# Norm statistics in two parts, HGRN's key multiplied later, and FFN one's norm in pieces, in a two-layer streaming trunk

## The chip, the cores and the metric

The kernel runs on one core of a Trainium2 chip. The metric is the device time of one execution in microseconds, as the median of several runs. The engines are named as in the profile: PE is TensorE, DVE is VectorE, ACT is ScalarE, POOL is GpSimd, SP is SyncE, which here only issues DMAs.

## The reference

Two groups of frames share all weights: a prompt of 1024 new frames and a sample of 32 frames that continues a running stream. Each passes a Mamba-2 SSD layer and an HGRN2 layer, and a SwiGLU FFN behind each. All numbers are float32.

```python
def rmsnorm(x, w):
    y = x * lax.rsqrt(jnp.mean(x * x, axis=-1, keepdims=True) + NORM_EPS)
    return y * w

# SSD mixer, cut: proj = h @ in_w; z, xbc, dt from proj; causal conv and silu on xbc; y from the chunked scan
yg = (y + D_skip * xs) * silu(z)
yg = rmsnorm over groups of 512 of yg, times gnorm_w
out = yg @ out_w

# HGRN mixer, cut: q, f, i, g = split(h @ in_w); forget = lb + (1 - lb) * sigmoid(f); k = 1 - forget
b = jnp.cumsum(log(forget), axis=1)          # in each chunk
qe, ke = q * jnp.exp(b), k * jnp.exp(-b)
sc = jnp.where(mask, qe @ ke.T, 0.0)
o = sc @ i + qe @ S
S = jnp.exp(last) * S + (k * jnp.exp(last - b)).T @ i
out = (rmsnorm per head of o * silu(g)) @ out_w

# trunk, for layer 0 (SSD) and layer 1 (HGRN)
x = x + mixer(rmsnorm(x, norm_w[layer]))
x = x + swiglu(rmsnorm(x, ffn_norm_w[layer]), w_gate, w_up, w_down)
# at the end
y = rmsnorm(x, final_norm_w)
```

D_MODEL is 1024, the FFN's hidden width 2816, the SSD has 32 heads of 64 in 4 groups, HGRN 8 heads of 128.

## The kernel before

The residual x lies in SBUF transposed, features on partitions, as eight tiles `acc[h][m]` of 128 features for each half `h`. Half 0 is 512 frames, half 1 the other 512 and the 32 of the sample (544, in two blocks of 272). In the profile `fixed` is the one large tile that holds x, the constants and the small buffers.

A product of float32 matrices is made of three passes (`product`, L346 to L348): weight and data are each split into a high part (`wh`, `xh`) and the rest (`wl`, `xl`). ACT rounds the high part, DVE subtracts. A result tile collects in one of five PSUM banks named `mm`, and DVE adds it into x (`accumulate`, shown as `fixed<-mm,fixed`). Scores, transposes and norm sums use three PSUM banks named `sc`.

A norm of x has two steps. The statistic (`rstd_of`, called for x by `x_stat` or by `norm`): ACT squares each of the eight tiles, DVE adds them up in `sq`, PE multiplies the sum by a matrix of ones (L369), ACT makes rsqrt as Exp(-0.5 Ln). Then for each tile the norm piece: DVE multiplies x by weight and statistic (`xf`), ACT rounds (`xn`), DVE subtracts.

**SSD layer.** Eight units (two halves, four groups) run one after another. A unit's frames go through `ssd_chunk` in chunks of 128, and tasks stand between the chunks: the z products (`ssd_z`), and the four out-projections (`ssd_out`) of the unit before. In the last unit the tasks are the four z products, then the whole norm of half 0 for FFN one (`norm`, in a high priority of 600), the four out-projections of unit six, and two first pieces of FFN one. The first four tasks (`PRE`) stand ahead of the chunks, the rest is dealt out over the chunks.

**HGRN layer.** Sixteen units (half, head). While unit i is scored, the projections of unit i+1 are made, in the order f, q, v, g. `hgrn_f` makes the log forget gate and its running sum, `hep` = exp(d) and `hem` = exp(-d), and the key `hk` = k times `hem`; `hgrn_q` makes `hq` = q times `hep`. `hgrn_scores` (L885) multiplies key and query, transposes the key and the value (L888) and copies them to `hkt` and `hvt`; `hgrn_states` (L908, L921) carries the state `hS`; `hgrn_outputs` (L933, L935) makes the output `ho`, whose own norm uses L367. Every second unit the out-projection of the two heads before (`hgrn_out`, products on `hy`) stands in between. In units (0,3) and (1,3) the last task is `x_stat` of the other half.

**FFN.** `ffn_half` runs over slabs of 256 hidden columns, in groups; the out-projections of a group are made within the next one. Its `hook`, called once in group one, is `x_stat` of the other half.

The order of instructions on each engine is made by the framework's scheduler, which starts from the program order and the priorities; each engine then runs its list in order and waits at an instruction until its inputs are there. The numbers behind names such as `hk_21829` in the lists below are the scheduler's.

Of the kernel before, what the change touches and what calls it, by code (L numbers as in the profile page):

```python
# [17 lines left out]
D = 1024  # L18
KD = D // P
# [29 lines left out]
def trunk_kernel(ctx, tc, x_prompt, x_sample, state_ssd, cache_conv, state_hgrn,  # L49
# [70 lines left out]
    def tt(out, a, b, op, eng=None):  # L120
        keep((eng or V).tensor_tensor(out=out, in0=a, in1=b, op=op))  # L121
# [593 lines left out]
    def ssd_layer(after, ws):  # L715
# [13 lines left out]
        for i, (h, g) in enumerate(units):  # L729
# [5 lines left out]
            if i + 1 < len(units):  # L735
                nh, ng = units[i + 1]
                if nh != h:
                    r = []
                    ps_ = [lambda m=m: norm_pieces(1, C_SSDN, xns[1], ((0, LEN[1]),), r[0])[m]() for m in range(KD)]
                    tasks = zs[:2] + [lambda: r.append(half_two_norm())] + zs[2:] + mixed(outs[:4], ps_) + \  # L740
                        [half_two_dt] + outs[4:]
                ct = ssd_conv_tasks(nh, ng, us[i + 1])
                tasks += ct[:EARLY]
                late = ct[EARLY:]
            else:
                tasks = zs + after[:1] + outs + after[1:]
            if i == 0:
# [8 lines left out]
            if h:  # L756
# [8 lines left out]
                act(Ss, ps, AF.Copy)  # L765
            nch = len(CHUNKS[h])
            loads = chunk_loads(h, g, 0, h == 0)
            for t in tasks[:PRE]:
# [54 lines left out]
    def hgrn_f(h, e, u):  # L823
# [27 lines left out]
        act(em[:, :L], d[:, :L], AF.Exp, scale=-1.0)  # L851
        tt(k[:, :L], k[:, :L], em[:, :L], MUL)
        u.update(k=k, ep=ep, ec=ec)

    def hgrn_q(h, e, u):
        L = LEN[h]
        q = T("ys", "hq")
        hgrn_proj(h, e, 0, silu2(q))
        stt(q[:, :L], q[:, :L], 0.5, u["ep"][:, :L], MUL, MUL)
        u["q"] = q  # L860

# [128 lines left out]
    def hgrn_layer(after):  # L990
# [7 lines left out]
        for i, (h, e) in enumerate(units):  # L998
# [21 lines left out]
            else:  # L1020
                tasks += after[1:2] + [states] + after[2:] + [outputs, rstd, gate]
            if (h, e) == (0, 3):
                tasks.append(lambda: r.append(x_stat(1, st[2])))
            if (h, e) == (0, 4):
                pieces = norm_pieces(1, C_HGN, xns[1], ((0, LEN[1]),), r[0], XN2)
            if (h, e) in ((0, 4), (0, 5), (0, 6)):
                tasks = mixed(tasks, pieces[:3])
                pieces = pieces[3:]
            if (h, e) == (1, 3):
                tasks.append(lambda: r.append(x_stat(0, st[3])))  # L1030
            if (h, e) == (1, 4):
# [19 lines left out]
    def x_stat(h, keep):  # L1051

        return rstd_of([acc[h][m][:, :LEN[h]] for m in range(KD)], BLK[h], 1.0 / D, LEN[h], keep)

# [220 lines left out]
    def ffn_half(layer, h, xn, tx, first, hook, tail, extra=()):  # L1275
# [5 lines left out]
        for gi, ng in enumerate(groups):  # L1281
            hid = []
            for i in range(ng):
# [4 lines left out]

                def gate(s=s + i, g=g, before=before, gi=gi):
                    yield from ffn_gate(layer, h, s, xn, tx, g)  # L1290
                    for d in before:
                        run(ffn_outs(*d))
                    if gi == 1 and before:
                        hook()
                    if gi and extra:
                        extra.pop(0)()
# [8 lines left out]
    def mixer_ffn(mixer, layer, wc, nxt):  # L1305
# [3 lines left out]
        h0, h1 = [ffn_head(layer, 0, s, xn[0]) for s in range(HEAD)]  # L1309
        if nxt:  # L1310
            entry = lambda: norm(0, wc, xn[0], XN)
        else:
            entry = lambda r: norm_pieces(0, wc, xn[0], BLK[0], r)
        rest = mixer([entry] + h0[:2])
        tc0 = x_combos(0, xn[0], tx[0])
# [3 lines left out]
        r = []  # L1319
        due = ffn_half(layer, 0, xn[0], tx[0], HEAD, lambda: r.append(x_stat(1, st[2])), [2])  # L1320
        kept = unsplit()
# [6 lines left out]
        if not nxt:  # L1328
            for q in range(2):
                wrow.append(st[2 + q][:, :512])  # L1330
                dma(wrow[q], final_norm_w[q * 512:(q + 1) * 512].unsqueeze(0).to_broadcast([P, 512]))
            done = [lambda g=g: finish(g, lambda: psum_mm((2, 3, 4))) for g in groups_of(0, 0, H1)]
        due = ffn_half(layer, 1, xn[1], tx[1], 1, lambda: r.append(nxt and x_stat(0, st[3])),
                       [2] if nxt else [1, 1], done)
        return due, r[0]

# [166 lines left out]
```

## Time and profile before

| | |
|---|---|
| median of 3 runs | 2859.85 us (2859.65 to 2860.43) |
| the profiled execution | 2858.78 us |
| its span in the trace | 2856.8 us |
| matmuls on PE | 19676 |
| granted TensorE clock, mean | 0.999 |

The profile has one row for a group of instructions: its line in the kernel, engine, operation, output and inputs by name, shape and count. The trace's timeline has one row for an instruction, or for some in a row of one form: start in us from the beginning of the span, duration, engine, line, and in brackets the idle time of the engine just before it with the instruction that ended it. Matmuls overlap in the pipeline, so that the duration of one is longer than the distance to the next.

### The profile page before, as it was taken

The page shows a single profiled execution, that of the slowest core. Times are in us where ns is not written, and L with a number is a line of the kernel's source. Part 1 is how long each engine was busy: PE and PEld are TensorE (multiplying, and loading weights), DVE is VectorE, ACT ScalarE, POOL GpSimd, SP SyncE. Part 2 cuts the span into 40 slices and gives each one's busy share as a digit, 9 for nine tenths or more (in the row PEclk, how much of TensorE's full clock was granted, in tenths as well). Part 3 has the DMA queues.
Part 4 walks back from the last instruction along what each step waited for, and adds up shares of the span by engine and source line. Part 5 has one row for each costly group of instructions (what it writes and reads, how often), then busy time and mean ns, then how long its engine had stood idle before and what let it go on. Part 6 is the DMA issues. An engine that isn't in the chain of part 4 may idle for free.

```text
span 2856.8 us, 48826 instructions
## 1 busy us (share of the span) xinstructions
PE 2826.3 (99%) x19676; PEld 2609.1 (91%) x19676; DVE 2132.9 (75%) x3663; ACT 1561.0 (55%) x2842; POOL 43.8 (2%) x158
## 2 busy tenths in 40 slices
PE   8999999999999999999999999999999999999998
PEld 8777788999989999999999888999988999999998
DVE  6887887787787877797777556656668877787776
ACT  6665655564653744466444666656554644455544
POOL 0000000000100000000000000000000000000000
PEclk9999999999999999999999999999999999999999
DMA  6443334444322333323333223222222332433332
GB/s 181 116 115 109 97 99 113 113 114 103 106 80 92 111 104 96 111 82 100 101 97 105 74 59 89 75 80 78 75 89 88 112 96 89 122 96 104 108 93 69
DMA packets 394516, 281.54 MB, mean 99 GB/s; under 512 B 16289, under 2 KB 382514, under 8 KB 394290
## 3 DMA queue, kind: packets, MB, share of 16 engines
q1 hardware_dynamic: 394274, 278.42, 33.6%
q8 instruction: 154, 2.52, 0.4%
q14 instruction: 72, 0.59, 0.1%
q10 hardware_dynamic: 16, 0.00, 0.0%
HBM read 270.57 MB, written 7.82 MB: 97 GB/s over the span
## 4 chain that ended last, share of the span: by engine, by line
PE 91%; DVE 5%; ACT 2%; issue 1%; DMA 1%; SPq 0%; POOL 0%; DVEq 0%; ACTq 0%; POOLq 0%
PE mm L346 18%; PE mm L348 18%; PE mm L347 18%; PE mm L1148 5%; PE mm L1146 5%; PE mm L1147 5%; PE sc L1148 4%; PE sc L1147 4%; PE sc L1146 4%; PE sc L661 1%; PE sc L650 1%; PE sc L647 1%; PE mm L1424 1%; DVE fixed L121 1%; PE sc L624 1%
## 5 line engine op out<-in xcount | busy, mean ns | idle before, releaser
L118 ACT ACTIVATE wh<-raw 128x512 fp32r<-128x512 f32 (+1 forms) x687 | 555.3, 816 | 599.1 <-PE mm L347 495.3
L346 PE MATMUL mm<-xn,wh 128*128 128x272 f32 (+2 forms) x1552 | 522.1, 337 | 2.3 <-ACT pre L118 1.3
L348 PE MATMUL mm<-xn,wl 128*128 128x272 f32 (+2 forms) x1552 | 516.6, 333 | 1.7 <-DVE wl L121 1.7
L347 PE MATMUL mm<-xn,wh 128*128 128x272 f32 (+2 forms) x1552 | 515.6, 333 | 0.0
L121 DVE TENSOR_TENSOR wl<-raw,wh 128x1024 fp32r<-128x1024 f32 (+1 forms) x307 | 373.0, 1217 | 147.3 <-ACT wh L118 118.2
L121 DVE TENSOR_TENSOR fixed<-mm,fixed 128x272 f32<-128x272 f32 (+3 forms) x504 | 259.6, 525 | 186.0 <-PE mm L348 179.7
L346 PE MATMUL mm<-fh,wh 128*128 128x272 f32 (+1 forms) x992 | 322.4, 326 | 0.3 <-ACT fh L118 0.2
L347 PE MATMUL mm<-fl,wh 128*128 128x272 f32 (+1 forms) x992 | 322.5, 326 | 0.0
L348 PE MATMUL mm<-fh,wl 128*128 128x272 f32 (+1 forms) x992 | 322.5, 326 | 0.0
L346 PEld LDWEIGHTS mm<-xn,wh 128*128 128x128 f32 x1552 | 291.5, 188 | 33.0 <-issue 2.9
L348 PEld LDWEIGHTS mm<-xn,wl 128*128 128x128 f32 x1552 | 291.4, 188 | 31.6 <-DVE wl L121 2.1
L347 PEld LDWEIGHTS mm<-xn,wh 128*128 128x128 f32 x1552 | 291.9, 188 | 27.7 <-issue 1.0
L121 DVE TENSOR_TENSOR wh<-raw,wh 128x512 fp32r<-128x512 f32 x380 | 256.3, 686 | 40.1 <-ACT wh L118 37.0
L1146 PE MATMUL mm<-th,wh 128*128 128x272 f32 (+1 forms) x912 | 260.5, 286 | 0.1
L1148 PE MATMUL mm<-th,wh 128*128 128x272 f32 (+1 forms) x912 | 259.9, 285 | 0.2 <-DVE wh L121 0.2
L1147 PE MATMUL mm<-tl,wh 128*128 128x272 f32 (+1 forms) x912 | 259.7, 285 | 0.0
L346 PEld LDWEIGHTS mm<-fh,wh 128*128 128x128 f32 x992 | 186.2, 188 | 16.4 <-ACT fh L118 1.9
L348 PEld LDWEIGHTS mm<-fh,wl 128*128 128x128 f32 x992 | 186.5, 188 | 15.4
L347 PEld LDWEIGHTS mm<-fl,wh 128*128 128x128 f32 x992 | 186.5, 188 | 15.0 <-DVE fl L121 0.2
L1146 PEld LDWEIGHTS mm<-th,wh 128*128 128x128 f32 x912 | 171.8, 188 | 1.9 <-ACT s L118 1.2
L1146 PE MATMUL sc<-xn,wh 128*128 128x272 f32 (+1 forms) x608 | 172.8, 284 | 0.5 <-ACT wh L118 0.5
L1148 PE MATMUL sc<-xn,wh 128*128 128x272 f32 (+1 forms) x608 | 173.1, 285 | 0.0
(310 smaller groups left out, 6642.6 us busy)
## 6 DMA issues: line engine op xcount, KB each, us to landing
raw<-in_ffn_w_gate_dram SPq DMA_DIRECT2D x88, 512.0 KB, 4.0
raw<-in_ffn_w_up_dram SPq DMA_DIRECT2D x88, 512.0 KB, 4.2
raw<-in_ffn_w_down_dram SPq DMA_DIRECT2D x88, 512.0 KB, 3.9
raw<-in_ssd_in_w_dram SPq DMA_DIRECT2D x80, 512.0 KB, 4.3
raw<-in_hgrn_in_w_dram SPq DMA_DIRECT2D x64, 512.0 KB, 4.0
cumB<-cumd SPq DMA_DIRECT2D x64, 256.0 KB, 4.2
raw<-in_ssd_out_w_dram SPq DMA_DIRECT2D x32, 512.0 KB, 3.4
raw<-in_hgrn_out_w_dram SPq DMA_DIRECT2D x16, 512.0 KB, 3.8
```

The source lines that it names most:

```text
L118: keep(A.activation(out=out, in_=in_, func=f, **kw))
L121: keep((eng or V).tensor_tensor(out=out, in0=a, in1=b, op=op))
L346: PE.matmul(ps[:, :bn], a, mh, start=(k == 0), stop=False)
L347: PE.matmul(ps[:, :bn], a, ml, start=False, stop=False)
L348: PE.matmul(ps[:, :bn], b, mh, start=False, stop=(k == n - 1))
L624: PE.transpose(ps[:n, j * P:(j + 1) * P], xs[j][:, xo:xo + n], ident)
L647: PE.matmul(y23[:, j, :n], S[:, j * P:(j + 1) * P], Cx, start=True, stop=True)
L650: PE.matmul(pp, Btok[:n, :], xw[:n, :], start=True, stop=True)
L661: PE.matmul(y13[r:r + 64, i // 2, :n], xdt[:n, i * 64:(i + 1) * 64], cums[i // 4][:n, i % 4, :n], start=True, stop=True)
L1146: PE.matmul(ps[:, :n], a, mh, start=(k == 0 and not more), stop=False, skip_group_check=True)
L1147: PE.matmul(ps[:, :n], a, ml, start=False, stop=False, skip_group_check=True)
L1148: PE.matmul(ps[:, :n], b, mh, start=False, stop=(k == 3), skip_group_check=True)
```

## The change

`x_stat` no longer runs as one piece. It returns a list of eight small steps, each squaring one tile (and adding it to the sum, which now lies in the buffer that later holds the statistic), and a function `mean` for the ones matmul (now L1077), Ln and Exp. The callers put the two apart:

- SSD: the squares of half 0 are mixed among unit six's tasks, `mean` stands at the start of unit seven, and the norm's eight pieces are mixed between unit six's four out-projections in unit seven, two after each, without the priority.
- HGRN: four squares among the tasks of unit e = 2, four among those of e = 3, `mean` at the end of e = 3, in both halves.
- FFN: the squares in group one, `mean` in group two.

Besides, `hgrn_f` no longer multiplies the key by exp(-d); `hgrn_q` does it behind its own multiplication. The same operations are computed on the same data; lines behind the edits move by some ten to thirty.

```diff
@@ ssd_layer
             else:
-                tasks = zs + after[:1] + outs + after[1:]
+                def entry(m):
+                    if not m:
+                        u["entry"] = after[0](u["r"])
+                    u["entry"][m]()
+                tasks = zs + mixed(outs, [lambda m=m: entry(m) for m in range(KD)]) + after[1:]
+            if i == len(units) - 2:
+                sq, mean = x_stat(0, st[0])
+                tasks = tasks[:PRE] + mixed(tasks[PRE:], sq)
...
+            if i == len(units) - 1:
+                u["r"] = mean()
             loads = chunk_loads(h, g, 0, h == 0)
@@ hgrn_f, hgrn_q
         act(em[:, :L], d[:, :L], AF.Exp, scale=-1.0)
-        tt(k[:, :L], k[:, :L], em[:, :L], MUL)
-        u.update(k=k, ep=ep, ec=ec)
+        u.update(k=k, ep=ep, em=em, ec=ec)
...
         stt(q[:, :L], q[:, :L], 0.5, u["ep"][:, :L], MUL, MUL)
+        k = u["k"]
+        tt(k[:, :L], k[:, :L], u["em"][:, :L], MUL)
@@ hgrn_layer
-            if (h, e) == (0, 3):
-                tasks.append(lambda: r.append(x_stat(1, st[2])))
+            if e in (2, 3):
+                if e == 2:
+                    sq, mean = x_stat(1 - h, st[2 + h])
+                tasks = mixed(tasks, sq[:4])
+                sq = sq[4:]
+                if e == 3:
+                    tasks.append(lambda mean=mean: r.append(mean()))
...
-            if (h, e) == (1, 3):
-                tasks.append(lambda: r.append(x_stat(0, st[3])))
@@ x_stat
-        return rstd_of([acc[h][m][:, :LEN[h]] for m in range(KD)], BLK[h], 1.0 / D, LEN[h], keep)
+        L = LEN[h]
+
+        def squares(m):
+            sq = keep if m == 0 else T("n", "sq")
+            act(sq[:, :L], acc[h][m][:, :L], AF.Square)
+            if m:
+                tt(keep[:, :L], keep[:, :L], sq[:, :L], ADD)
+
+        def mean():
+            for (b0, bn) in BLK[h]:
+                ps = psum_sc()
+                PE.matmul(ps[:, :bn], ones, keep[:, b0:b0 + bn], start=True, stop=True)
+                act(keep[:, b0:b0 + bn], ps[:, :bn], AF.Ln, bias=epsc[:, 0:1], scale=1.0 / D)
+            act(keep[:, :L], keep[:, :L], AF.Exp, scale=-0.5)
+            return keep
+        return [lambda m=m: squares(m) for m in range(KD)], mean
@@ ffn_half, in gate
-                    if gi == 1 and before:
-                        hook()
+                    if gi in (1, 2) and i == 0:
+                        hook[gi - 1]()
@@ mixer_ffn
-        if nxt:
-            entry = lambda: norm(0, wc, xn[0], XN)
-        else:
-            entry = lambda r: norm_pieces(0, wc, xn[0], BLK[0], r)
-        rest = mixer([entry] + h0[:2])
+        rest = mixer([lambda r: norm_pieces(0, wc, xn[0], BLK[0], r)] + h0[:2])
...
-        due = ffn_half(layer, 0, xn[0], tx[0], HEAD, lambda: r.append(x_stat(1, st[2])), [2])
+        sq, mean = x_stat(1, st[2])
+        due = ffn_half(layer, 0, xn[0], tx[0], HEAD, (lambda: run(sq), lambda: r.append(mean())), [2])
...
-        due = ffn_half(layer, 1, xn[1], tx[1], 1, lambda: r.append(nxt and x_stat(0, st[3])),
-                       [2] if nxt else [1, 1], done)
-        return due, r[0]
+        sq, mean = x_stat(0, st[3])
+        hooks = (lambda: run(sq), lambda: r.append(mean())) if nxt else (lambda: None,) * 2
+        due = ffn_half(layer, 1, xn[1], tx[1], 1, hooks, [2] if nxt else [1, 1], done)
+        return due, nxt and r[0]
```

How the scheduled order moves is shown at three places. The first is PE in HGRN's unit (1,3). Before, the ones matmul L369 stood among the out-projection's products (on `hy`), behind the f projection of unit (1,5):

```order
L346 MATMUL mm_17156<-hy_20104,wh_21056 128x272
L347 MATMUL mm_17156<-hy_20104,wh_21056 128x272
L348 MATMUL mm_17156<-hy_20104,wl_21057 128x272
L369 MATMUL sc_20923<-sq_20900,fixed 128x512
L885 MATMUL sc_20929<-hq_20686,hk_20644 128x128 x4
L888 MATMUL sc_20930<-fixed,hk_20644 128x128 x4
```

Now it stands, as L1077, behind the last product of the g projection (weights `wh_20854`) and ahead of the f projection of unit (1,5) (`wh_20946`), the scores (now L895) and transposes (now L898) with it:

```order
L346 MATMUL mm_17153<-h_18961,wh_20854 128x272
L347 MATMUL mm_17153<-l_18962,wh_20854 128x272
L348 MATMUL mm_17153<-h_18961,wl_20855 128x272
L1077 MATMUL sc_20917<-fixed 128x512
L895 MATMUL sc_20923<-hq_20693,hk_20649 128x128 x4
L898 MATMUL sc_20924<-fixed,hk_20649 128x128 x4
L346 MATMUL mm_17154<-h_18309,wh_20946 128x272
```

So the ones matmul, the scores and the first transposes moved ahead of the f projection and of the out-projection.

The second place is DVE in HGRN's unit (1,6), where the gates of unit (1,7) are made beside an out-projection. Before, the key's multiplication by `hem` stood ahead of a step of unit (1,6)'s state (`hS`):

```order
L124 SCALAR_TENSOR_TENSOR xf_21846<-fixed 128x512
L121 TENSOR_TENSOR hk_21829<-hk_21829,hem_21842 128x544
L921 TENSOR_SCALAR hS_21856<-fixed 128x128
L121 TENSOR_TENSOR xn<-xf_21846,xn 128x512
L121 TENSOR_TENSOR fixed<-hS_21856,sc_21851 128x128
L121 TENSOR_TENSOR fixed<-mm_17159,fixed 128x272
L921 TENSOR_SCALAR hS_21856<-fixed 128x128
```

Now the state's steps (now L931) and the accumulates (`fixed<-mm`) go on without it:

```order
L124 SCALAR_TENSOR_TENSOR xf_21839<-fixed 128x512
L931 TENSOR_SCALAR hS_21849<-fixed 128x128
L121 TENSOR_TENSOR fixed<-mm_17155,fixed 128x272
L121 TENSOR_TENSOR fixed<-hS_21849,sc_21844 128x128
L121 TENSOR_TENSOR xn<-xf_21839,xn 128x512
L931 TENSOR_SCALAR hS_21849<-fixed 128x128
L121 TENSOR_TENSOR fixed<-mm_17151,fixed 128x272
L121 TENSOR_TENSOR fixed<-mm_17152,fixed 128x272
L121 TENSOR_TENSOR fixed<-mm_17153,fixed 128x272
L121 TENSOR_TENSOR fixed<-mm_17154,fixed 128x272
L121 TENSOR_TENSOR fixed<-mm_17155,fixed 128x272
L121 TENSOR_TENSOR fixed<-mm_17151,fixed 128x272
```

The multiplication follows two rows further on, behind seven accumulates that stand in a row.

The third place is DVE in the last SSD unit. Before, the norm's `xf` and `xn` rows stood together, with two accumulates only near their end:

```order
L124 SCALAR_TENSOR_TENSOR xf_8347<-fixed,rstd_8330 128x512
L124 SCALAR_TENSOR_TENSOR xf_8351<-fixed,rstd_8330 128x512
L124 SCALAR_TENSOR_TENSOR xf_8355<-fixed,rstd_8330 128x512
L121 TENSOR_TENSOR xn<-xf_8347,xn 128x512
L121 TENSOR_TENSOR xn<-xf_8351,xn 128x512
L124 SCALAR_TENSOR_TENSOR xf_8359<-fixed,rstd_8330 128x512
L121 TENSOR_TENSOR xn<-xf_8355,xn 128x512
L124 SCALAR_TENSOR_TENSOR xf_8363<-fixed,rstd_8330 128x512
L121 TENSOR_TENSOR xn<-xf_8359,xn 128x512
L121 TENSOR_TENSOR fixed<-mm_8401,fixed 128x272
L121 TENSOR_TENSOR xn<-xf_8363,xn 128x512
L121 TENSOR_TENSOR fixed<-mm_8415,fixed 128x272
```

Now four `xn` stand ahead of the first chunk's mask product (`fixed<-sc_8284`), behind the last z products:

```order
L124 SCALAR_TENSOR_TENSOR z_8222<-z_8222,mm_8223 128x272
L121 TENSOR_TENSOR xn<-xf_8395,xn 128x512
L121 TENSOR_TENSOR xn<-xf_8399,xn 128x512
L121 TENSOR_TENSOR xn<-xf_8521,xn 128x512
L121 TENSOR_TENSOR xn<-xf_8525,xn 128x512
L121 TENSOR_TENSOR fixed<-sc_8284,fixed 128x128
L124 SCALAR_TENSOR_TENSOR xf_8647<-fixed 128x512
L124 SCALAR_TENSOR_TENSOR z_8222<-z_8222,mm_8250 128x272
L121 TENSOR_TENSOR xdt_8292<-sc_8287,fixed 128x512
L121 TENSOR_TENSOR xw_8293<-sc_8287,fixed 128x512
```

and of the other four pieces each stands among a chunk's accumulates:

```order
L121 TENSOR_TENSOR fixed<-fixed,sc_8445 128x512
L121 TENSOR_TENSOR fixed<-mm_8465,fixed 128x272
L124 SCALAR_TENSOR_TENSOR xf_8651<-fixed 128x512
L121 TENSOR_TENSOR fixed<-mm_8479,fixed 128x272
L121 TENSOR_TENSOR wl_8714<-raw_8711,wh_8713 128x1024
L121 TENSOR_TENSOR fixed<-mm_8493,fixed 128x272
L121 TENSOR_TENSOR xn<-xf_8651,xn 128x512
L124 SCALAR_TENSOR_TENSOR xf_8773<-fixed 128x512
L121 TENSOR_TENSOR fixed<-mm_8507,fixed 128x272
L121 TENSOR_TENSOR fixed<-sc_8536,fixed 128x128
```

So the accumulates no longer stand behind a row of norm pieces, and the first half of the pieces moved to the z products and the first chunk.

More of the change, by code (lines that the diff above doesn't have):

```diff
@@ L1287, in ffn_half, with gate @@
                     before, due = due, []
-                def gate(s=s + i, g=g, before=before, gi=gi):
+                def gate(s=s + i, g=g, before=before, gi=gi, i=i):
                     yield from ffn_gate(layer, h, s, xn, tx, g)
```

## The prediction

> **What bounds the kernel now.** The first view is the page's busy times and the chain of work that ended last.
>
> ```profile
> PE 2826.3 (99%) x19676; PEld 2609.1 (91%) x19676; DVE 2132.9 (75%) x3663; ACT 1561.0 (55%) x2842; POOL 43.8 (2%) x158
> PE 91%; DVE 5%; ACT 2%; issue 1%; DMA 1%; SPq 0%; POOL 0%; DVEq 0%; ACTq 0%; POOLq 0%
> ```
>
> TensorE (PE) sets the time. The change removes no matmul, so it can only give back time in which PE stands idle, or add to it. The second view is therefore the list of PE's waits; its columns are the waiting instruction, what released it, the total in us, how often, and the longest.
>
> ```profile
> PE sc L369 <- DVE sq L121: 4.9, 4, 1.8
> PE mm L212 <- DMA fixed<-in_x_prompt_dram: 4.5, 2, 4.1
> PE mm L346 <- DVE fixed L121: 2.2, 2, 1.3
> PE sc L935 <- DVE hS L921: 1.0, 1, 1.0
> PE sc L908 <- ACT hvt L118: 0.8, 1, 0.8
> ```
>
> L369 is the ones-matrix matmul of a norm: it waits until VectorE (DVE) has summed the eight squares. Of its four waits one belongs to an SSD gate, which the change leaves alone. L212 is the first load of the input and is not touched either. The other rows are. The third view, PE's timeline, puts each at its time (start, length, instruction, and in brackets the idle time before it and what ended that):
>
> ```profile
> 790.72 0.39 PE L346 MATMUL mm<-yh,wh 128*128 128x272 f32 x1 [1.30 <-DVE fixed L121]
> ...
> 961.57 1.18 PE L369 MATMUL sc<-sq,fixed 128*128 128x272 f32 x4 [1.48 <-DVE sq L121]
> ...
> 1712.41 0.95 PE L369 MATMUL sc<-sq,fixed 128*128 128x272 f32 x3 [1.22 <-DVE sq L121]
> ...
> 1929.18 0.39 PE L346 MATMUL mm<-hy,wh 128*128 128x272 f32 x1 [0.86 <-DVE fixed L121]
> ...
> 1994.94 1.12 PE L369 MATMUL sc<-sq,fixed 128*128 128x512 f32 x2 [1.83 <-DVE sq L121]
> ...
> 1999.28 0.28 PE L346 MATMUL mm<-hy,wh 128*128 128x272 f32 x1
> 1999.41 0.29 PE L347 MATMUL mm<-hy,wh 128*128 128x272 f32 x1
> 2000.51 0.38 PE L908 MATMUL sc<-hvt,hkt 128*128 128x128 f32 x1 [0.81 <-ACT hvt L118]
> ...
> 2080.38 0.49 PE L935 MATMUL sc<-hq,hS 128*128 128x128 f32 x2 [1.04 <-DVE hS L921]
> ```
>
> Seven waits: 1.30 + 1.48 + 1.22 + 0.86 + 1.83 + 0.81 + 1.04 = 8.54 us. A wait costs more than its bracket. The rows at 1999.28 and 1999.41 start 0.13 us apart although each lasts 0.29; the bracket counts from the end, the next product would have started 0.16 earlier. So the seven cost 8.54 + 7 x 0.16 = 9.7 us. That is the most the change can fetch from them.
>
> **The statistics (L369).** What fills the time before these waits is one burst of the eight squares' additions:
>
> ```profile
> 1989.28 2.28 DVE L121 TENSOR_TENSOR sq<-sq,sq 128x512 f32<-128x512 f32 x3
> 1991.47 1.22 DVE L121 TENSOR_TENSOR wl<-raw,wh 128x1024 fp32r<-128x1024 f32 x1
> 1992.61 2.28 DVE L121 TENSOR_TENSOR sq<-sq,sq 128x512 f32<-128x512 f32 x3
> ...
> 1701.95 0.65 ACT L118 ACTIVATE sq<-fixed 128x544 f32<-128x544 f32 x1
> ...
> 1982.78 0.63 ACT L118 ACTIVATE sq<-fixed 128x512 f32<-128x512 f32 x1
> ```
>
> Each addition stands 0.76 us after the last; with the split weights between, the last ends at 1994.89, and PE, idle for 1.83 us by then, starts the ones matmul at 1994.94. After the change there are the same eight squares, seven additions, one ones matmul, Ln and Exp, but the squares come in pieces. For HGRN's unit (1,3) four squares lie in the unit before and four in the unit; the last stands on ScalarE (ACT) where the row at 1982.78 stands now (behind the Ln of the unit's own norm), and its addition follows it on a DVE that is then idle:
>
> ```profile
> 1704.57 0.75 DVE L124 SCALAR_TENSOR_TENSOR ho<-ho,fixed,rstd 128x512 f32<-128x512 f32 x1 [3.75 <-ACT rstd L118]
> ...
> 1985.41 0.79 DVE L124 SCALAR_TENSOR_TENSOR ho<-ho,fixed,rstd 128x544 f32<-128x544 f32 x1 [3.73 <-ACT rstd L118]
> 1704.51 0.40 PE L346 MATMUL mm<-xn,wh 128*128 128x512 f32 x1
> ...
> 1985.81 0.29 PE L346 MATMUL mm<-h,wh 128*128 128x272 f32 x1
> ```
>
> So the sum is ready near 1982.78 + 0.63 + 0.76 = 1984.2, and PE, which now comes to the ones matmul right after the 48 g products (the one at 1985.81 is the 49th), gets there near 1985.8. Cover: 1.6 us. The wait goes: -1.99 with its start. HGRN's unit (0,3), where PE waited at 1712.41, reads the same: last square 1701.95, sum near 1703.4, the 24 g products over by 1704.51 (the row is the 25th), cover 1.1 us: -1.38. In FFN one (961.57) the squares now lie a whole group of weight slabs ahead of the ones matmul, some 480 products in the order: -1.64. The statistics of the last SSD unit, of FFN one's second half and of FFN two have no wait now: moving them gives 0; what they could cost is bounded below. In the SSD layer the order leaves the additions about where they were.
>
> **hvt (2000.51).** Right behind, ACT does a table load and the statistic's Exp just ahead of the copy that PE waits for:
>
> ```profile
> 1998.04 1.28 ACT L118 ACT_TABLE_LOAD   x1
> 1999.34 0.63 ACT L118 ACTIVATE fixed<-fixed 128x512 f32<-128x512 f32 x1
> 1999.87 0.58 ACT L118 ACTIVATE hvt<-sc 128x512 f32<-128x512 f32 x1
> ```
>
> These still precede it, but in the order the matmul on hvt now has 39 of the f products between it and the transposes that hvt copies: 39 x 0.125 = 4.9 us against the 1.28 + 0.63 + 0.58 = 2.5 shown. That goes: -0.97.
>
> **HGRN's key times exp(-d) later.** Two of PE's waits stand behind this one multiplication, since DVE, in order, stops at it until exp(-d) is there:
>
> ```profile
> 1927.86 0.72 DVE L121 TENSOR_TENSOR hk<-hk,hem 128x544 f32<-128x544 f32 x1 [1.27 <-ACT hem L118]
> ...
> 2079.40 0.73 DVE L121 TENSOR_TENSOR hk<-hk,hem 128x544 f32<-128x544 f32 x1 [1.15 <-ACT hem L118]
> 2080.05 0.28 DVE L921 TENSOR_SCALAR hS<-fixed 128x128 f32<-128x128 f32 x1
> ```
>
> At 2080.05 the state step that PE waits for starts only after it; at 1929.18 it is an accumulate. The order moves the multiplication behind a row of accumulates in the units with out-projections: 1.27 + 0.64 and 1.15 + 0.64 us of DVE leave the chain, more than the waits of 0.86 and 1.04. Both go: -1.02 and -1.20. Who needs the key next:
>
> ```profile
> L885 PE MATMUL sc<-hq,hk x128: 270/275/275, 1585.9 to 2107.8; 128*128 128x128 f32 x128
> L121 DVE TENSOR_TENSOR hk<-hk,hem x16: 686/707/727, 1576.9 to 2079.4; 128x512 f32<-128x512 f32 x8, 128x544 f32<-128x544 f32 x8
> ```
>
> From the first multiplication to the first score are 9.0 us, from the last one about 28: a few us later is covered.
>
> **FFN one's norm between out-projections.** Now the eight xf and eight xn pieces are one burst at high priority, and the accumulate that frees PE's bank stands in it:
>
> ```profile
> L124 DVE SCALAR_TENSOR_TENSOR xf<-fixed,rstd 128x512 f32<-128x512 f32 x8 | 5.6, 746 | 0.0
> L121 DVE TENSOR_TENSOR xn<-xf,xn 128x512 fp32r<-128x512 f32 x8 | 5.2, 684 | 0.0
> ...
> 781.52:791.80 10.28, 8.98 (x73) 8.76 (x72) 10.28 (x19) 9.23 (x23) 0.00 (x0) 1.00 0.35 91
> 791.80:801.00 9.20, 9.18 (x73) 7.70 (x72) 8.79 (x20) 2.24 (x7) 0.00 (x0) 1.00 0.16 33
> 801.00:810.80 9.80, 9.80 (x83) 8.87 (x82) 8.62 (x14) 5.39 (x12) 0.53 (x1) 1.00 0.37 100
> 810.80:820.50 9.70, 9.70 (x61) 7.57 (x60) 9.31 (x15) 3.78 (x13) 0.00 (x0) 1.00 0.25 72
> ```
>
> Behind length and PE, PEld, the third busy time is DVE's: 10.28 of 10.28 us beside the burst. Afterwards four xf stand among the z products and the rest goes two pieces after each out-projection: -1.46. But DVE is full here. These four stretches hold 37.0 us of DVE work in 39.0; without the four xf that leave (4 x 0.7 = 2.8), 34.2 remain for 37.5 us of PE: a tenth is free, on average.
>
> **New waits.** No row shows them. Bounds: below, -0.4, if the one small wait left in this stretch, on ACT's fh, goes as well:
>
> ```profile
> 844.66 0.72 PE L346 MATMUL mm<-fh,wh 128*128 128x512 f32 x2 [0.25 <-ACT fh L118]
> ```
>
> Above, +5: at each of seven places PE waits for one DVE operation of 0.72 us. I take +1.5, six waits of the size of this row, which is the nearest in kind; most of it in the last SSD unit, where four xn now stand ahead of a chunk's mask product. ACT gets four more table loads (two in each HGRN unit with a statistic), DVE one instruction row, SP some swaps of neighbouring loads, POOL nothing; ACT is 55% busy and the loads lie beside products, so nothing for these.
>
> **Sum.** -1.46 - 1.64 - 1.38 - 1.02 - 1.99 - 0.97 - 1.20 = -9.7; +1.5 gives -8.2. The profiled execution took 2858.78 us (2856.8 of it the span); it would take 2850.6. It stands 1.07 under the median of the runs, so the forecast is 2859.85 - 8.2 = **2851.7**.
>
> **The rivals.** *The waits come back one place on.* DVE's work is the same, and a wait on the sum may become one on an accumulate. Then only the three L369 waits go (5.0 us), and 2 us return: 2859.85 - 3.0 = 2856.9. For it speaks DVE's load of 88 to 100% in the SSD rows above; against it the idle 3.75 and 3.73 us in HGRN. 0.20.
>
> *Table loads on the path.* If each of the four added loads delays what PE waits for by its 1.30 us (1998.04 to 1999.34), +5.2: 2856.9. Against it: the 4.9 us of products ahead of hvt. 0.04. [...]
>
> *DVE becomes the bound in the last SSD unit (slower).* It decides once DVE's work in a chunk exceeds PE's 9.2 to 9.8 us there. Then each of the eight pieces holds an accumulate as the burst did at 790.72: 8 x 1.46 = 11.7, and that wait's own gain is lost: -8.2 + 1.5 + 11.7 = +5.0, 2864.9; if each holds the chunk's own products too, twice the price: +16.7, 2876.6. For it: 9.31 of 9.70 in the last row above, where no norm piece stands. Against it: the 10% average. 0.09, of which 0.07 beyond 0.2%.
>
> *It does not do what it says.* A scheduler places the rows; the lists of both orders show the moves, but an engine's real waits could be on other things, and the gain nil: 2859.9. 0.05.
>
> **Numbers.** Forecast 0.62. A measurement of this kernel can tell about 0.2% (5.7 us) from no change: faster needs less than 2854.1. Faster 0.62, within 0.31 (0.20 + 0.04 + 0.02 + 0.05), slower 0.07. Low end: all seven waits, the fh wait and the runs' spread of 0.2: 2859.85 - 9.7 - 0.4 - 0.2 = 2849.6. High end 2858.4: the first rival with half of its gain.
>
> **What will show it.** The row L369 <- DVE sq (now the mean's matmul) should fall from four waits to the gate's one; 790.72, 1929.18, 2000.51 and 2080.38 should be without idle time. Wrong, if the waits on accumulates grow past 3 us, if the mean's matmul waits in HGRN, or if PE's idle time between 770 and 830 grows.

## The result: 0.25% faster, close to the forecast

| | kernel before | changed kernel |
|---|---|---|
| median of 9 runs each, us | 2859.03 (2857.39 to 2860.43) | 2852.09 (2850.33 to 2852.80) |
| profiled execution: time, span, us | 2858.78, 2856.8 | 2852.09, 2850.2 |
| sum of PE's idle times in the trace, us | 23.2 | 17.7 |

The ratio of the times is 0.9975 with a 95% interval of 0.9967 to 0.9983; a second set of runs (11 and 7) gave 0.9971, 0.9961 to 0.9982. The forecast was 2851.7, a change of -8.2 us; the medians differ by -6.9 and the profiled spans by -6.6. That the two times agree to 0.4 us is partly luck: the median of before from which the forecast started (2859.85, three runs) lies 0.8 above that of nine, and the table of stages below shows errors of opposite sign that cancel.

The page of the changed kernel has the same bound and the same amount of work:

```profile
PE 2825.2 (99%) x19676; PEld 2609.1 (92%) x19676; DVE 2131.4 (75%) x3663; ACT 1563.5 (55%) x2846; POOL 44.0 (2%) x158
```

ACT has four instructions more, the table loads (111 beside 107, of 1.28 us each). The list of PE's waits (waiting instruction, releaser, total us, times, longest) is where the kernels differ. Four of its rows:

```profile
PE sc L898 <- DVE hsc L901: 1.5, 1, 1.5
...
PE mm L346 <- DVE fixed L121: 1.0, 2, 0.5
...
PE mm L1174 <- ACT s L118: 0.5, 2, 0.3
...
PE sc L369 <- DVE sq L121: 0.4, 1, 0.4
```

The statistics' row has fallen from four waits and 4.9 us to the gate's one of 0.4, and the rows on hS and hvt are gone. But there are rows that did not exist before (the transposes L898 wait for the masked scores hsc, and products of FFN for `s`, a copy that ACT makes), and the row on accumulates, `DVE fixed`, still counts two waits, half as long. PE's timeline of the changed kernel puts the new ones at their times:

```profile
1984.31 0.66 PE L898 MATMUL sc<-fixed,hv 128*128 128x128 f32 x4 [1.53 <-DVE hsc L901]
...
2000.14 0.39 PE L346 MATMUL mm<-hy,wh 128*128 128x272 f32 x1 [0.49 <-DVE fixed L121]
...
1032.23 0.39 PE L1174 MATMUL mm<-th,wh 128*128 128x256 f32 x1 [0.26 <-ACT s L118]
...
2307.55 0.39 PE L1174 MATMUL mm<-th,wh 128*128 128x256 f32 x1 [0.28 <-ACT s L118]
```

A twin of the second stands at 2074.32. In the last SSD unit PE has no idle time at all; the columns of this row are the stretch, its length, and the busy time of PE, PEld, DVE, ACT and POOL, then clock, DMA share and GB/s:

```profile
770.00:820.00 50.00, 50.00 (x400) 43.96 (x399) 46.98 (x88) 25.04 (x62) 0.52 (x1) 1.00 0.29 79
```

For the rest, the program is cut into four stages by starts of matmuls in PE's timeline, since the beginning varies from run to run (last section). SSD goes from the first to the last product on yh, FFN one from there to the first on hsc, HGRN from the first to the last on hy, FFN two from there to the last matmul. (From the first hsc to the first hy is 48.0 to 48.2 us in every profile.)

| us | SSD | FFN one | HGRN | FFN two and end |
|---|---|---|---|---|
| before | 760.33 | 699.74 | 533.16 | 668.33 |
| changed | 757.42 | 699.03 | 529.65 | 668.94 |
| difference | -2.91 | -0.71 | -3.51 | +0.61 |
| by the forecast's terms | -1.46 | -1.64 | -6.56 | 0 |

The forecast had +1.5 of new waits beside these terms. The last stage lies between 668.2 and 669.5 over all twelve profiles, and at 668.94 and 669.45 in two of the changed kernel, so its +0.61 is not clear of the scatter.

### Where the new waits come from

**The wait at 1984.31.** These are rows of PE, ACT and DVE around it, from the timelines of the changed kernel:

```profile
1979.30 1.02 PE L1077 MATMUL sc<-fixed 128*128 128x512 f32 x2
1980.16 1.05 PE L895 MATMUL sc<-hq,hk 128*128 128x128 f32 x8
1981.05 0.60 PE L898 MATMUL sc<-fixed,hk 128*128 128x128 f32 x4
...
1982.38 1.28 ACT L118 ACT_TABLE_LOAD   x1
1983.67 0.69 ACT L118 ACTIVATE fixed<-sc,fixed 128x512 f32<-128x512 f32 x1
...
1982.39 1.23 DVE L121 TENSOR_TENSOR wl<-raw,wh 128x1024 fp32r<-128x1024 f32 x1 [0.16 <-ACT wh L118]
1983.53 0.72 DVE L901 COPY_PREDICATED hsc<-fixed,sc 128x512 f32<-128x512 uint32 x1
```

The small results share three PSUM banks (`sc`). The mean's matmul now takes the first at 1979.30, right ahead of the scores and of the key's transposes, and holds it until its logarithm has read it, which ACT does at 1983.67, behind a table load. The value's transposes need a fourth bank, and the first to come free is that of the scores, at the end of hsc (1983.53 + 0.72 = 1984.25). Theory: the bank that the mean holds is the cause, and hsc only the release that came first.

**The waits at 2000.14 and 2074.32.** ACT and DVE ahead of the first:

```profile
1997.66 0.64 ACT L118 ACTIVATE hem<-hlg 128x544 f32<-128x544 f32 x1
1998.20 0.61 ACT L118 ACTIVATE xn<-xf 128x512 fp32r<-128x512 f32 x1
...
1998.85 0.69 DVE L121 TENSOR_TENSOR xn<-xf,xn 128x512 fp32r<-128x512 f32 x1 [0.94 <-ACT xn L118]
1999.46 0.28 DVE L931 TENSOR_SCALAR hS<-fixed 128x128 f32<-128x128 f32 x1
1999.66 2.17 DVE L121 TENSOR_TENSOR fixed<-mm,fixed 128x272 f32<-128x272 f32 x6
```

DVE no longer stops at hk times hem. It stops one row on, at a norm piece's xn, whose copy on ACT stands behind hem all the same. A row of accumulates queues behind it, and PE waits for the first of them. Theory: the stop has moved from the key to the norm piece, and shrunk.

### The profile page after: what moved, and what is told of

Same layout as the page of the kernel before. It is cut to its first block, busy times and chain, and to the rows that moved or that the text cites. A ratio compares the mean times of both kernels' runs of the same rounds, so it can differ in the third digit from the quotient of the medians.

```text
span 2850.2 us, 48834 instructions
## 1 busy us (share of the span) xinstructions
PE 2825.2 (99%) x19676; PEld 2609.1 (92%) x19676; DVE 2131.4 (75%) x3663; ACT 1563.5 (55%) x2846; POOL 44.0 (2%) x158
## 4 chain that ended last, share of the span: by engine, by line
PE 91%; DVE 5%; ACT 2%; DMA 1%; issue 1%; SPq 0%; POOL 0%; DVEq 0%; ACTq 0%; POOLq 0%
PE mm L346 19%; PE mm L348 19%; PE mm L347 19%; PE mm L1176 5%; PE mm L1174 5%; PE mm L1175 5%; PE sc L1176 4%; PE sc L1174 4%; PE sc L1175 4%; PE sc L661 1%; PE sc L650 1%; PE sc L647 1%; PE mm L1450 1%; DVE fixed L121 1%; ACT wh L118 1%
```

## Experiments

The first four undo or keep one part each. Besides the single time, each is read by its stages, because a single time holds a start that varies by up to 2.5 us. The code shown is the part of each edit that matters. A cost "by starts" is the distance from one matmul's start to the next, less the distance without a wait.

**The key alone.** The kernel before with nothing but the key's move (`em` is also handed on in `u`):

```
@@ hgrn_f
-        tt(k[:, :L], k[:, :L], em[:, :L], MUL)
@@ hgrn_q, at its end
+        k = u["k"]
+        tt(k[:, :L], k[:, :L], u["em"][:, :L], MUL)
```

> The kernel before with only the key's multiplication moved. Each wait has its own cause (theory): PE's waits of 0.86 us near 1929 and of 1.04 near 2080 go, the other five of the seven stay, and the wait of 0.5 us on an accumulate near 2078, which DVE's norm piece behind exp(-d) makes in the changed kernel, is there. Span 2856.8 - 1.0 - 1.2 + 0.55 = 2855.1 us. Rival (DVE only waits for exp(-d) at another instruction, and PE with it): waits of 0.8 to 1.0 us on accumulates at the same two places, span within 0.5 of 2856.8.

Measured: 2856.14 beside 2858.16 for before. HGRN is 531.95, 1.2 shorter than before; the expected terms made 1.7. The waits at 1929 and 2080 are gone; in the place of the second stands one on an accumulate. PE's timeline:

```profile
959.41 0.95 PE L369 MATMUL sc<-sq,fixed 128*128 128x272 f32 x3
...
1327.01 0.39 PE L1147 MATMUL mm<-th,wh 128*128 128x272 f32 x1 [0.82 <-ACT s L118]
...
2078.92 0.39 PE L346 MATMUL mm<-hy,wh 128*128 128x272 f32 x1 [0.50 <-DVE fixed L121]
```

The first two rows were not expected. This kernel has FFN one in the order of before, and yet its ones matmul, which idled 1.48 us there, has no bracket here (its gap is 0.04), while 0.82 us appear at 1327. So that wait is not the same in every run; FFN one is 699.03 here, as in the changed kernel. The traces show where it came from. DVE waits for a weight tile from memory ahead of the squares' last additions, first in the profile of before, then here:

```profile
949.22 0.69 DVE L121 TENSOR_TENSOR fixed<-raw,raw 128x512 f32<-128x512 f32 x1 [2.15 <-DMA raw<-in_ffn_w_gate_dram]
```

```profile
947.06 0.69 DVE L121 TENSOR_TENSOR fixed<-raw,raw 128x512 f32<-128x512 f32 x1 [0.76 <-DMA raw<-in_ffn_w_gate_dram]
```

DVE's wait is 1.39 us longer in the first. From there to the last addition DVE runs the same 19 instructions in both, without any idle time, and the ones matmul waits 1.44 us longer. So in the profile of before the wait was a weight tile that landed late; the undivided statistic only left no room for it.

**The key early.** The changed kernel with the multiplication put back into hgrn_f (the same lines, reversed).

> The changed kernel with the key's multiplication put back into the gates' part. Theory: the waits of 0.86 and 1.04 us on DVE at the two places (near 1923 and 2074) come back, one of the two new accumulate waits of 0.5 goes with them: span 2850.2 + 1.0 + 1.2 - 0.55 = 2851.9 us; the wait of 1.53 us on hsc stays. Rival: no change beyond 0.5 us.

Measured: 2851.50, and HGRN 531.44, 1.8 longer than in the changed kernel. The time alone hides this, since this run's first yh product came 0.64 us earlier, and FFN one and two took 0.9 and 0.7 less. PE's timeline shows the two old waits and a third of their kind, at 1998.89:

```profile
1922.28 0.39 PE L346 MATMUL mm<-hy,wh 128*128 128x272 f32 x1 [0.87 <-DVE fixed L121]
...
1998.89 0.49 PE L944 MATMUL sc<-hq,hS 128*128 128x128 f32 x2 [1.05 <-DVE hS L930]
...
2073.40 0.49 PE L944 MATMUL sc<-hq,hS 128*128 128x128 f32 x2 [1.05 <-DVE hS L930]
```

Both half-microsecond waits on accumulates are gone, where one was expected to go. Idle time: 0.87 + 1.05 + 1.05 - 0.49 - 0.50 = +2.0. So the key's move gives 1.2 us by itself and 1.8 beside the rest, against 2.22 in the forecast.

**HGRN's statistics whole.** The changed kernel with squares and mean at the end of units (0,3) and (1,3):

```
-            if e in (2, 3):
-                if e == 2:
-                    sq, mean = x_stat(1 - h, st[2 + h])
-                tasks = mixed(tasks, sq[:4])
-                sq = sq[4:]
-                if e == 3:
-                    tasks.append(lambda mean=mean: r.append(mean()))
+            if e == 3:
+                sq, mean = x_stat(1 - h, st[2 + h])
+                tasks += sq
+                tasks.append(lambda mean=mean: r.append(mean()))
```

> The changed kernel with HGRN's two statistics as one piece at the end of their unit, as before. Theory: PE's waits on the ones matmul come back (1.2 us in the first half, 1.8 in the second, and 0.8 on hvt), the new wait of 1.53 us on hsc goes, since it is the early mean that holds a bank: span 2850.2 + 1.38 + 1.99 + 0.97 - 1.69 = 2852.9 us. Rival (hsc's wait comes from the key's place, not from the mean): it stays, span 2854.5.

Measured: 2853.28, and HGRN 532.10, 2.45 longer. PE's timeline:

```profile
1707.07 0.73 PE L1074 MATMUL sc<-fixed 128*128 128x272 f32 x2 [1.11 <-DVE fixed L121]
...
1986.75 1.12 PE L1074 MATMUL sc<-fixed 128*128 128x512 f32 x2 [1.34 <-DVE fixed L121]
...
1992.37 0.82 PE L918 MATMUL sc<-hvt,hkt 128*128 128x128 f32 x5 [0.74 <-ACT hvt L118]
```

All three old waits are back, the sum's and hvt's, and the one on hsc is gone. The cutting of the statistic therefore caused both the gain and the wait at 1984.31.

**The norm whole in the last SSD unit.** The changed kernel with FFN one's squares, mean and pieces in one burst at high priority, as before (`whole` runs the squares, the mean and the eight pieces, and the squares leave unit six):

```
-                tasks = zs + mixed(outs, [lambda m=m: entry(m) for m in range(KD)]) + after[1:]
+                tasks = zs + [whole] + outs + after[1:]
```

> The changed kernel with FFN one's norm for the first half as one piece of high priority behind the z products, as before. Theory: the wait of 1.30 us on an accumulate near 790 comes back with two hidden ones of 0.16 and 0.24 us in the next chunk and 0.25 on fh: span 2850.2 + 1.46 + 0.4 + 0.4 = 2852.5 us. Rival (DVE is full there either way and only the place of the wait differs): within 0.5 us of 2850.2.

Measured: 2853.19, and SSD 760.29, 2.87 longer. PE's timeline:

```profile
790.20 0.39 PE L346 MATMUL mm<-yh,wh 128*128 128x272 f32 x1 [1.33 <-DVE fixed L121]
...
844.10 0.97 PE L346 MATMUL mm<-fh,wh 128*128 128x512 f32 x3 [0.27 <-ACT fh L118]
```

So this part, statistic and pieces together, is worth 2.9 us, twice the forecast's term for the pieces. Beside 1.46 for the wait at 790 there are 0.41 for that on fh (a case that the forecast had only as a bound), and, by starts, 0.16 and 0.24 us at 796.30 and 797.25 in the profile of before, where DVE was late by less than the matmul ahead lasts (0.27 and 0.33 us), so that hardly a bracket shows it (0.02 us at the second). Some 0.6 us are spread over steps too small to assign.

**FFN's statistics whole.** The changed kernel with squares and mean both in group one of each FFN half:

```
-                    if gi in (1, 2) and i == 0:
-                        hook[gi - 1]()
+                    if gi == 1 and i == 0:
+                        hook[0]()
+                        hook[1]()
```

> The changed kernel, but in both FFN halves the squares and the mean of the norm are issued together in group one, as before the change. The forecast's step on FFN one: the wait of the mean's matmul on the last square's sum (1.48 us at 961.57 in the profile of before) comes back, and the small new waits of the gate products on s in FFN one (0.42 and 0.23) and two (0.44) go. FFN one, from the last yh product to the first hsc matmul, is 699.0 us in the profile of the changed kernel and would be about 699.0 + 1.6 - 0.65 = 700.0; the span grows by about 0.5 us. Rival: that wait depends on a near miss of the DMA or DVE order in one profile (the key-alone kernel, with the old FFN order, had 0.04 us there, and 0.82 us at another place): then FFN one stays within 0.3 us of 699.0, with a wait of under 0.5 us in the mean's matmul.

Measured: 2850.57 beside 2859.30 for before (with an early start). FFN one is 700.39, 1.4 longer, but not by the wait named: the mean's matmul at 952.33 does not wait, since the last addition, which stands earlier in DVE's order than in the kernel before, ended at 948.92. The waits are of another kind, on ACT's s (a copy out of PSUM beside the split of weights):

```profile
968.04 0.38 PE L1174 MATMUL mm<-th,wh 128*128 128x256 f32 x1 [0.47 <-ACT s L118]
...
1323.49 0.40 PE L1174 MATMUL mm<-th,wh 128*128 128x272 f32 x1 [0.82 <-ACT s L118]
```

Neither theory holds as written. Eight profiles with the changed kernel's FFN one lie between 698.15 and 699.11; the ninth, the next experiment's, has the same order of matmuls there and is 700.27. The three with the undivided statistic are 699.74, 699.03 and 700.39. The medians differ by 0.7, and one order alone spreads over 2.1. That this part gains anything in most runs is not shown.

**DVE loaded.** The changed kernel with two adds that nothing reads behind each norm piece of the last SSD unit:

```
                     u["entry"][m]()
+                    for _ in range(2):
+                        tt(st[1][:, :512], u["r"][:, :512], u["r"][:, :512], ADD)
```

> The changed kernel with two more VectorE adds of 128x512 behind each of the eight norm pieces in the last SSD unit (16 x 0.68 us = 10.9 us of DVE work that nothing reads). It measures the room that the forecast gave DVE there: a tenth of 37.5 us, 3.3 us. By that estimate 10.9 - 3.3 = 7.6 us come onto PE as waits of accumulates' readers, and the SSD stage, first to last yh product, grows from 757.4 to about 765. Rival: the five banks and the units behind the stretch absorb more than the average says, since DVE stands still for 9.7 us between 820 and 860: then under 3 us, 757.4 to 760.4. If DVE had been the bound already (the slower rival of the forecast), all 10.9 would show: 768.3.

Measured: 2855.07, and SSD 759.58, only 2.2 longer for 10.9 us of DVE work. (The time grew by 3.0; FFN one took 1.2 longer in this run, for reasons not assigned.) One wait makes most of it. DVE, then PE:

```profile
766.66 2.86 DVE L121 TENSOR_TENSOR fixed<-fixed 128x512 f32<-128x512 f32 x4
...
772.60 2.49 DVE L121 TENSOR_TENSOR xn<-xf,xn 128x512 fp32r<-128x512 f32 x4
...
776.15 0.68 DVE L121 TENSOR_TENSOR xw<-sc,fixed 128x512 f32<-128x512 f32 x1
...
776.98 1.10 PE L650 MATMUL sc<-xw,fixed 128*128 128x512 f32 x2 [1.69 <-DVE xw L121]
```

It stands where the forecast feared a new wait: four xn ahead of a chunk's first products. Without the load they fit; with it xw is late and PE idles for 1.69 us, 1.85 by starts. The scheduler put twelve of the sixteen adds (8.2 us) between 757 and 772, beside the z products, where DVE of the changed kernel was busy for 20.73 of the 30 us from 740 to 770, and only four (2.7 us) among the chunks' accumulates, at 801 to 813, where they cost at most the other 0.3. So the expected 7.6 came from a wrong place for the load. In the chunks the forecast's room of 3.3 us has been used to 2.7 and held; whether more fits there was not tried.

**The mean before rstd.** The changed kernel with the mean right ahead of the unit's own rstd, all squares before it:

```
-                tasks = mixed(tasks, sq[:4])
-                sq = sq[4:]
-                if e == 3:
-                    tasks.append(lambda mean=mean: r.append(mean()))
+                if e == 2:
+                    tasks = mixed(tasks, sq[:4])
+                    sq = sq[4:]
+                else:
+                    tasks = mixed(tasks[:5], sq) + [lambda mean=mean: r.append(mean())] + tasks[5:]
```

> The changed kernel, but in the HGRN units (0,3) and (1,3) all squares stand before rstd and the norm's mean right before rstd instead of at the unit's end, so that its logarithm shares rstd's table load (two loads fewer per half) and its bank is free before the scores. Theory: the new wait of hv's transposes on hsc (1.53 us idle, 1.69 by starts, at 1984.31) comes from the mean's bank, which is held until its logarithm behind a table load of 1.28 us. Then it goes: HGRN, first to last hy product, falls from 529.65 to about 528.0, and the span by as much. Rival: the bank is not the cause, hsc is late by DVE's weight split: the wait stays at over 1 us. Second rival: the mean's matmul now waits for its own sum (1.4 us as before the change), or rstd's matmuls wait for a third bank: 529.5.

Measured: 2850.24, and HGRN 527.97, 1.68 shorter, the 1.69 of the wait. ACT, then PE, then DVE:

```profile
1974.34 1.28 ACT L118 ACT_TABLE_LOAD   x1
1975.63 0.69 ACT L118 ACTIVATE fixed<-sc,fixed 128x512 f32<-128x512 f32 x1
1976.22 0.48 ACT L118 ACTIVATE rstd<-sc,fixed 128x272 f32<-128x272 f32 x1
...
1981.63 0.60 PE L898 MATMUL sc<-fixed,hv 128*128 128x128 f32 x4
...
1984.19 0.74 DVE L901 COPY_PREDICATED hsc<-fixed,sc 128x512 f32<-128x512 uint32 x1
```

The mean's logarithm follows the load that rstd's needs anyway, its bank is free 4 us before the scores (1975.63 + 0.69 = 1976.32, beside 1980.30), and the transposes start without a bracket. The scores still go through the same copy on DVE, and that copy starts 2.56 us after the transposes, so the bank was the cause. This kernel also has two table loads fewer (four were expected), and beside the wait they saved nothing that shows (1.68 beside 1.69): the forecast's zero for loads beside products stands.

**The pieces late.** The changed kernel with the norm pieces of units (1,4) and (1,6) mixed only into the tasks behind the out-projections:

```
-                tasks = mixed(tasks, pieces[:3])
+                cut = 4 if outs else 0
+                tasks = tasks[:cut] + mixed(tasks[cut:], pieces[:3])
```

> The changed kernel, but in HGRN's units (1,4) and (1,6) the three norm pieces are mixed only into the tasks behind the out-projections. Theory: the two waits of hy products on accumulates (0.55 us by starts each, at 2000.14 and 2074.32) come from DVE standing still for 0.94 us at xn, behind hep and hem on ScalarE. Then both go: HGRN, first to last hy product, falls from 529.65 to about 528.55. Rival: DVE's load in these units is what binds, and the wait moves to a reader of q or of the outputs: 529.4 to 529.9. The wait at 1984.31 stays (1.5).

Measured: 2848.42 (with an early start), and HGRN 527.64, 2.0 shorter. DVE at the same place:

```profile
1995.47 1.85 DVE L121 TENSOR_TENSOR fixed<-mm,fixed 128x272 f32<-128x272 f32 x5
1997.63 0.44 DVE L121 TENSOR_TENSOR fixed<-mm,fixed 128x272 f32<-128x272 f32 x1 [0.30 <-PE mm L348]
1997.99 0.71 DVE L121 TENSOR_TENSOR hk<-hk,hem 128x544 f32<-128x544 f32 x1
```

DVE now waits for PE, not PE for DVE, and hem is there before the key needs it. Both waits are gone. That is 1.1 to 1.3 of the 2.0; the rest is not assigned. The run does not part two readings: it took away both DVE's stop of 0.94 us at xn and the 0.61 us of xn itself, and either alone is longer than the wait of 0.49.

**Both repairs, and the changed kernel beside them.**

> The changed kernel with both repairs of HGRN: the mean right before rstd, and the pieces of units (1,4) and (1,6) behind the out-projections. Alone they took 1.68 and 2.01 us from HGRN's 529.65. If they are independent, HGRN, first to last hy product, is 526.0 and the time 3.7 us under that of the changed kernel: about 2848.4 beside its 2852.1, and 2859.0 for the kernel before (ratio 0.9963). Rival: one takes the other's room on DVE or ScalarE, and HGRN is 527.0 or more.

> The changed kernel once more, on the same chip as the version with both repairs, so that the two can be set side by side: 2852.1 us, 0.9975 of the kernel before. The start of the program varies by over 2 us from run to run (the first transposes take 1.6 or 2.9 us in their profiles), so the single runs should scatter over 2850 to 2853, and the kernel before over 2857 to 2860.5.

Measured on one chip: 2848.14 (5 runs, 2846.17 to 2849.09) for both repairs, 2851.92 (7 runs, 2849.80 to 2852.48) for the changed kernel, 2859.19 (11 runs, 2857.08 to 2861.77) for before. The ratios to before are 0.9960 (0.9947 to 0.9974) and 0.9971 (0.9961 to 0.9982); the intervals overlap, but every run with both repairs was shorter than every run of the changed kernel. The stages are clearer: HGRN is 526.08 against 529.61, and SSD and FFN one agree to 0.14. The two repairs add up (1.68 + 2.01 = 3.69; measured 3.53), and PE's longest wait in HGRN is 0.14 us.

## Why the forecast was right, and where it was not

**The bound and the seven waits.** Right, but for FFN one (below). Busy time hardly changed, and the instructions that waited at the seven places (790.72, 961.57, 1712.41, 1929.18, 1994.94, 2000.51 and 2080.38 in the profile of before) have no idle time before them in the changed kernel. In HGRN the sums are ready 2.0 and 1.7 us ahead of their ones matmuls, where the forecast had 1.1 and 1.6. That a wait costs its bracket and 0.16 more is borne out at 1984.31, where a 128x272 product stands before it: 1.53 of idle time is 1.69 by starts. Behind the small matmul L968 at 2000.14 it is 0.06 to 0.16 more: 0.06 if that matmul's usual distance is the 0.21 between it and its twin, 0.16 if it is the 0.11 to its usual successor.

**New waits, +1.5: mis-sized, and in the wrong stage.** By starts they are 1.69 (1984.31), 0.55 to 0.65 twice (2000.14, 2074.32), 0.42 and 0.27 in FFN one, and 0.44 in FFN two: +3.9 to +4.1. The last three are not shown to come from the change, since the waits on s differ between runs of one order: the key alone, with the old order, has 0.82 us of them, and the list of before, in the same order, has none. The forecast expected most of them in the last SSD unit, where there are none. Its bounds of -0.4 and +5 took in the value. It missed two things that the order of the change showed: that the mean's matmul, moved ahead of the scores, takes one of three banks there, and that behind the key the next row on DVE was an xn waiting on the same engine.

**Gains not counted, -0.8.** The wait on fh (-0.41) and the two hidden delays at 796 and 797 (-0.40). Together: -9.66 + 3.92 - 0.81 = -6.55, or -6.35 with the higher price, beside -6.6 between the spans. That the sum closes is in part luck: the 0.6 us of SSD that no step explains is missing in it, and the other stages give back 0.3 to 0.5 more than it has. The forecast's total is luck in the same way: its seven terms are 1.45 us short in SSD, and 3.05 and 0.93 too high in HGRN and FFN one. The terms were taken from one profile of each kernel; as the next point shows, some of them belong to that profile.

**FFN one, -1.64: not a cost of the order.** The forecast took a wait of one profile as a cost of the order. It was a weight tile for which DVE waited 1.4 us longer than in the profile of the key alone, where the same order left PE waiting 0.04. The two profiles of the results differ by 0.71 in this stage, which lies within the 2.1 us that one order spreads over. The last addition now ends 66 us before its ones matmul, so a landing that late no longer delays it; how often one did before is not known.

**HGRN.** Forecast -6.56, measured -3.51: the new waits there are 2.8 to 3.0, and at most 0.26 is left over. The bank is shown as the cause of the first by the repair that took it away. For the two on accumulates the repair shows that the norm pieces make them, but not whether by DVE's stop or by their own work.

**The rivals.** *The waits come back one place on* was half right: in HGRN, not in SSD, and 2.8 us. *Table loads on the path*: the loads delay nothing of PE's directly. Of the changed kernel's idle times in HGRN three are over 0.1 us (1.53, 0.49 and 0.49), all ended by DVE, none by an ACT instruction behind a load. But one of them does stand in the chain that holds the mean's bank (1982.38 to 1983.67), a way to the path that the forecast did not see. *DVE becomes the bound*: it does not, and four fifths of a load of 10.9 us were still hidden, though three quarters of that load lay where DVE had room. *It does not do what it says*: the interval of the ratio does not reach 1, and undoing the parts in SSD and HGRN brought their waits back.

## What to carry to other kernels

Where a reduction is cut up so that nobody waits for its sum, look at what its last step then holds: here a bank of a ring of three, taken ahead of the scores, made the next user wait for somebody else's release (1.53 us at 1984.31). Beside rstd, behind one load that serves both logarithms, the same step left HGRN 1.68 us shorter. And where an engine in program order stops at an operand, ask whether the row behind that instruction waits for the same producer: with the key moved, DVE still stopped for 0.94 us at xn (1998.85), where the key early had it stop for 1.16 at the key (1997.91). Before a wait of one profile is counted as a gain, ask whether the order makes it or a transfer that happened to land late (here 2.15 us of DVE's waiting in one profile and 0.76 in another, with the same order there).

## What was not expected of the hardware

The start of these kernels varies by 2.5 us, from the beginning of the span to the first yh product, which is over a third of this change. PE's first transposes in the changed kernel, and in the one with the late pieces:

```profile
9.14 2.93 PE L404 MATMUL sc<-fixed 128*128 128x128 f32 x12 [1.54 <-DVE fixed L385]
```

```profile
8.91 1.61 PE L404 MATMUL sc<-fixed 128*128 128x128 f32 x12 [1.54 <-DVE fixed L385]
```

They are the same instructions in the same place. In the profile of before PE's transposes start 213 or 214 ns apart from 9.63 to 14.75 us after the start of the span, and 109 to 112 ns apart from 14.96 on; in that of the changed kernel the change falls between 13.78 and 14.13. In the late pieces the twelve above take 1.44 us up to the start of the next row (10.35), 120 ns each, where the changed kernel's take 2.72 (up to 11.86), 227 each. By PE's matmuls between 8 and 12 us FFN's statistics whole is like the late pieces (31 and 29), while before, the changed kernel, the mean before rstd and the key early have 15 or 16. The first yh product is at 137.3 us in the late pieces and at 137.1 in FFN's statistics whole, instead of 138.8 to 139.6. The clock column of the windows says 1.00 throughout in these six profiles, so only the spacing shows it. What sets the moment of the change is not shown by any run. The two profiles in which it comes early are the two with the early first yh product, some 2 us ahead of the others, and the stages behind it were compared here for that reason.
